# One decoder layer on one core: z and v projections with 512 output columns per matmul instead of 256

## The chip, the cores and the metric

The kernel runs on one core of a Trainium2 chip. The metric is the device time of one execution in microseconds (us). Five engines work side by side, each through its own queue in order: TensorE (PE in the profile, with its weight loads listed apart as PEld), VectorE (DVE), ScalarE (ACT), GpSimd (POOL) and SyncE (SP), which issues most transfers.

## The reference, cut to what matters

One layer of a hybrid decoder, 512 tokens by 1024 features, float32. One input projection of x gives q, k, v of 16 attention heads of 64, the gate z and the inputs x, B, C, dt of a Mamba-2 branch with 32 heads in 4 groups, and two branch gates. The change touches the two products whose results have tokens on the partitions:

```
proj = x @ w_in[l]
q, k, v, f_logit, z, xbc, dt_raw, gate_logit = jnp.split(proj, split_idx, axis=-1)
...
u = (y.reshape(bsz, seq, SSM_INNER) * jax.nn.silu(z.astype(jnp.float32))).reshape(bsz, seq, SSM_GROUPS, -1)
...
return jnp.einsum('bhqk,bhkd->bhqd', p, vh)
```

z has 2048 columns, 512 for each of the four Mamba groups; v has 1024 columns, 64 for each head. Behind the two branches come an output projection, a LayerNorm, a SwiGLU feed-forward part and a second LayerNorm.

## The kernel before

Each operand of a large product is split into hi + lo (float32r), and a product is three matmuls, hi·hi, hi·lo, lo·hi (`mm3`, lines 97 to 100), summed in PSUM. Weights come in chunks of 1024 values per partition: a transfer on SP's queue into `raw` (4 buffers), a copy on ACT that makes `whi`, a subtraction on DVE that makes `wlo` (3 buffers each; `load_w`, lines 85 to 95, both with high priority in the scheduler).

There are three forms of product. `gemm_ws` holds weights in the array and streams 512 tokens; it serves x, B, C, q, k, the gates and the feed-forward up and gate projections. `gemm_down` holds activations and streams 512 weight columns, one PSUM bank for each of the token tiles (128 tokens). `gemm_xs` (lines 118 to 132) also holds activations, but streams 256 weight columns; two token tiles share one PSUM bank, and it runs twice (`pair` 0 and 1) for the 512 columns of a Mamba group's z, and once for the 256 columns of v of four heads.

PSUM has eight banks: a ring `gps` of 3 for projections and a ring `cps` of 5 for transposes, scores and small products.

A scheduler sets the order of each engine's queue ahead of time. The stages: x is transposed tile by tile along with z of group 0; small parameters; B, C and x of group 0; for each group g a chain `group_y` (scan over four chunks) beside the projections of its neighbours, then z of group g (`group_z`, lines 248 to 257: tanh on ACT, one multiply on DVE per bank into `gz`), then `group_u` (lines 315 to 331: for each token tile y times gz, a sum of squares on ACT, a power on POOL, a scaling by DVE, four transposes on PE, a split). Then attention by groups of four heads (hg): q and k of the next group are projected (`att_qk`) while the heads of this group run, v of the group stands ahead of its heads (`att_v`, lines 370 to 379). A head (`att_head`) is scores (lines 390, 391) on PE, maximum (395) on DVE, exponential (397) on ACT, reciprocal and scaling (398, 399) on DVE, transposes (412) on PE, a split on ACT and DVE (65, 66), and the product with v (418) on PE. Rings of few buffers join the steps: the score bank, the transposed bank and the output bank all come from `cps`.

Of the kernel before, what the change touches and what calls it, by code (L numbers as in the profile page):

```python
# [9 lines left out]
F32 = mybir.dt.float32  # L10
F32R = mybir.dt.float32r
BF16 = mybir.dt.bfloat16
AF = mybir.ActivationFunctionType
ALU = mybir.AluOpType
# [23 lines left out]
def tile_hybrid_decoder_layer(  # L38
# [6 lines left out]
    """Operands of the large products are split exactly as hi + lo (float32r each); a product is  # L45
    hi*hi + hi*lo + lo*hi, accumulated in float32."""
# [21 lines left out]
    def gps():  # L68
        return psum.tile([P, T], F32, name="gps", bufs=3)

    def cps():
        return psum.tile([P, T], F32, name="cps", bufs=5)

    # SBUF slots by size (KB), shared over the phases of the layer
# [10 lines left out]
    def load_w(src, a, b, dst=None):  # L85
        """Weights [a * 128, b] to SBUF, split; hi and lo of each block of 128 rows."""
        raw = stream.tile([P, 1024], F32, name="raw", bufs=4)
        nc.sync.dma_start(out=raw.rearrange("p (a b) -> p a b", a=a), in_=src.rearrange("(a p) c -> p a c", p=P))
        if dst is None:
            dst = ([stream.tile([P, 1024], F32R, name="whi")], [stream.tile([P, 1024], F32R, name="wlo")])  # L90
        n = 1024 // len(dst[0])
        with tc.high_priority():
            for i, (hi, lo) in enumerate(zip(*dst)):
                split(hi, lo, raw[:, i * n:(i + 1) * n])
        return [[t[:, j * b:(j + 1) * b] for t in part for j in range(n // b)] for part in dst]
# [9 lines left out]
    def gemm_ws(w, c0, nk, rhs, evac, alloc=gps, n=T, chunks=None):  # L105
        """256 output features (two blocks of 128 partitions) x n tokens; weights stationary."""
# [11 lines left out]
    def gemm_xs(w, c0, lhs, evac, before=None):  # L118
        """512 tokens x 256 output features, tokens on partitions; activations stationary."""
        ps = [gps() for _ in range(2)]  # L120
        for half in range(2):
            hi, lo = ws_chunk(w, c0, half)
            for tt in range(NT):
                if before is not None and half == 0:
                    before(tt)
                o = ps[tt // 2][:, (tt % 2) * 256:(tt % 2 + 1) * 256]
                for k in range(4):
                    kt = half * 4 + k
                    mm3(o, lhs(kt, tt), (hi[k], lo[k]),
                        kt == 0 and tt % 2 == 0, kt == KD - 1 and tt % 2 == 1)  # L130
        for i in range(2):
            evac(i, ps[i].rearrange("p (t c) -> p t c", t=2))
# [4 lines left out]
    def gemm_down(chunk, nk, lhs, tts, half, evac, alloc, tail=0, tail_dst=None):  # L137
        """Tokens tts x 512 output features, tokens on partitions; the last `tail` pairs of k token by token."""
# [18 lines left out]
    def new_act():  # L157
        """A [1024 features, 512 tokens] operand: features on partitions, hi and lo."""
# [8 lines left out]
    def transpose_in(a, src, tt):  # L167
        """Token tile src [128 tokens, 1024] into the operand a."""
# [79 lines left out]
    def group_z(g, before=None):  # L248
        gz = big("gz")
        for pair in range(2):  # L250
            def evac(i, ps, pair=pair):
                th = slot("th").rearrange("p (t c) -> p t c", t=2)
                nc.scalar.activation(out=th, in_=ps, func=AF.Tanh, scale=0.5)
                nc.vector.scalar_tensor_tensor(out=gz[:, 2 * i:2 * i + 2, pair * 256:(pair + 1) * 256], in0=th,
                                               scalar=1.0, in1=ps, op0=ALU.add, op1=ALU.mult)
            gemm_xs(w_in, C_Z + g * 512 + pair * 256, lhs_x, evac, before if pair == 0 else None)
        return gz

    def group_y(g, st):
# [8 lines left out]
        for c in range(NT):  # L268
# [5 lines left out]
            for hf in range(2):  # L274
                # exp(min(acum[l] - acum[s], 0)) * cb[l, s], zero where l < s
# [94 lines left out]
    def att_v(hg):  # L370
        vt = slot("xtok", (P, NT, 4, P), F32R)

        def evac(i, ps):
            sv = ps.rearrange("p t (h d) -> p t h d", h=4)
            hi = vt[:, 2 * i:2 * i + 2, :, 0:64]
            nc.scalar.copy(out=hi, in_=sv)
            nc.vector.tensor_tensor(out=vt[:, 2 * i:2 * i + 2, :, 64:128], in0=sv, in1=hi.bitcast(F32), op=ALU.subtract)
# [3 lines left out]
    def att_head(h, qk, vt, of):  # L381
# [4 lines left out]
        for i in range(NT):  # L386
# [7 lines left out]
            # pt = -(s + mask), with its least value: the negated maximum  # L394
# [109 lines left out]
    # log1p(exp(-|v|)) = 2 atanh(s), s = e / (2 + e) <= 1/3  # L504
# [96 lines left out]
    for hg in range(4):  # L601
# [3 lines left out]
        vt = att_v(hg)  # L605
# [142 lines left out]
    banks = [gps(), gps(), gps(), cps()]  # L748
# [30 lines left out]
```

## Time and profile before

| what | value |
|---|---|
| median of three runs | 1175.7 us (1175.45 to 1175.77) |
| span of the profiled execution | 1171.8 us |
| time of the runs around that span | 3.9 us (1175.7 - 1171.8); the profiled execution's own time is not given apart |
| PE busy | 1145.6 us, 98% |
| DVE busy | 679.9 us, 58% |
| ACT busy | 468.4 us, 40% |
| POOL busy | 99.1 us, 8% |
| DMA | 112.66 MB, 96 GB/s |

The busy time of PE is the union of its matmuls, whose ends are modelled and overlap: a matmul listed with 0.39 us may be followed by the next 0.23 us after its start. So distances from start to start are the measure of what a matmul costs, not its listed duration.

### The profile page before, as it was taken

The numbers are of one execution on the slowest core, as the hardware profiler recorded it, in microseconds if no ns is written. First come the engines' busy times: TensorE is split into PE (matmuls) and PEld (weight loads), VectorE is DVE, ScalarE is ACT, GpSimd is POOL, SyncE is SP. The second block draws the span as 40 slices with busy tenths as digits, with TensorE's granted clock in tenths as the row PEclk, the third lists the DMA queues.
The fourth block names the chain that finished last, engine by engine and source line by source line (L and its number), as shares of the span: only waits on it lengthen the run. The fifth ranks groups of instructions, "written<-read, shape, count | busy, mean of one in ns | idle before, by whom it ended". The sixth has DMA issues, their size and how long they took to land.

```text
span 1171.8 us, 15180 instructions
## 1 busy us (share of the span) xinstructions
PE 1145.6 (98%) x5966; PEld 959.3 (82%) x5966; DVE 679.9 (58%) x1110; ACT 468.4 (40%) x826; POOL 99.1 (8%) x137
## 2 busy tenths in 40 slices
PE   7999999999999999999999999999999999999997
PEld 6887779879778888888787888888888888888886
DVE  3579964883786565877878344546443433432426
ACT  3376763453442434655656352302322322322120
POOL 2003130030131001120200000010000000000001
PEclk9999999999999999999999999999999999999999
DMA  8343243233231232222221355502333333333221
GB/s 244 90 129 126 73 126 90 74 117 100 83 99 55 91 90 73 57 72 73 56 73 55 90 162 161 169 31 72 108 90 105 94 92 106 90 100 98 91 72 73
DMA packets 99576, 112.66 MB, mean 96 GB/s; under 512 B 4820, under 2 KB 84912, under 8 KB 99376
## 3 DMA queue, kind: packets, MB, share of 16 engines
q1 hardware_dynamic: 97024, 107.03, 30.6%
q10 hardware_dynamic: 1152, 4.19, 1.0%
q0 software_dynamic: 1328, 0.46, 0.3%
q8 instruction: 47, 0.77, 0.3%
q14 instruction: 25, 0.20, 0.1%
HBM read 109.38 MB, written 2.16 MB: 95 GB/s over the span
## 4 chain that ended last, share of the span: by engine, by line
PE 86%; DVE 7%; ACT 2%; POOL 2%; issue 2%; DMA 1%; SPq 0%; DVEq 0%; ACTq 0%; POOLq 0%
PE gps L100 20%; PE gps L98 20%; PE gps L99 20%; PE cps L98 6%; PE cps L100 6%; PE cps L99 6%; PE cps L418 1%; PE cps L287 1%; PE cps L412 1%; DMA raw<-in_w_in_dram 1%; DVE wlo L66 1%; DVE t_ul L66 1%; PE cps L244 1%; PE cps L296 1%; PE cps L304 1%
## 5 line engine op out<-in xcount | busy, mean ns | idle before, releaser
L66 DVE TENSOR_TENSOR wlo<-raw,whi 128x1024 fp32r<-128x1024 f32 x171 | 210.1, 1228 | 316.6 <-ACT whi L65 316.5
L65 ACT CAST whi<-raw 128x1024 fp32r<-128x1024 f32 x171 | 179.6, 1050 | 401.2 <-PE gps L99 134.3
L99 PE MATMUL gps<-xl,whi 128*128 128x512 f32 (+1 forms) x648 | 253.6, 391 | 0.0
L98 PE MATMUL gps<-xh,whi 128*128 128x512 f32 (+1 forms) x648 | 252.6, 390 | 0.1
L100 PE MATMUL gps<-xh,wlo 128*128 128x512 f32 (+1 forms) x648 | 251.6, 388 | 0.0
L98 PEld LDWEIGHTS gps<-xh,whi 128*128 128x128 f32 x648 | 122.1, 188 | 23.3 <-issue 0.7
L100 PEld LDWEIGHTS gps<-xh,wlo 128*128 128x128 f32 x648 | 122.4, 189 | 21.9
L99 PEld LDWEIGHTS gps<-xl,whi 128*128 128x128 f32 x648 | 122.2, 189 | 21.6 <-issue 0.2
L98 PE MATMUL gps<-whi,xh 128*128 128x256 f32 (+1 forms) x400 | 116.1, 290 | 2.7 <-ACT xh L65 2.7
L99 PE MATMUL gps<-wlo,xh 128*128 128x256 f32 (+1 forms) x400 | 115.8, 290 | 0.2 <-DVE wlo L66 0.2
L100 PE MATMUL gps<-whi,xl 128*128 128x256 f32 (+1 forms) x400 | 115.9, 290 | 0.0
L98 PEld LDWEIGHTS gps<-whi,xh 128*128 128x128 f32 x400 | 77.4, 194 | 4.3 <-ACT xh L65 3.5
L99 PEld LDWEIGHTS gps<-wlo,xh 128*128 128x128 f32 x400 | 77.4, 193 | 1.4 <-DVE wlo L66 0.5
L100 PEld LDWEIGHTS gps<-whi,xl 128*128 128x128 f32 x400 | 77.4, 194 | 0.6
L98 PE MATMUL cps<-xh,whi 128*128 128x512 f32 (+1 forms) x176 | 66.8, 380 | 0.0
L100 PE MATMUL cps<-xh,wlo 128*128 128x512 f32 (+1 forms) x176 | 66.8, 379 | 0.0
L99 PE MATMUL cps<-xl,whi 128*128 128x512 f32 (+1 forms) x176 | 66.8, 379 | 0.0
L676 POOL TENSOR_TENSOR mv<-mv,neghalf 128x1 f32<-128x1 f32 x8 | 9.2, 1154 | 569.8 <-DVE mv L675 569.8
L198 DVE SCALAR_TENSOR_TENSOR t_v<-gps,cw,t_v 128x511 f32<-128x511 f32 (+2 forms) x72 | 53.4, 744 | 4.3 <-ACT t_v L195 3.5
L100 PE MATMUL gps<-t_uh,wlo 128*128 128x512 f32 x128 | 51.4, 402 | 0.0
L99 PE MATMUL gps<-t_ul,whi 128*128 128x512 f32 x128 | 51.0, 398 | 0.3 <-DVE t_ul L66 0.3
L98 PE MATMUL gps<-t_uh,whi 128*128 128x512 f32 x128 | 50.3, 393 | 0.0
(560 smaller groups left out, 1913.2 us busy)
## 6 DMA issues: line engine op xcount, KB each, us to landing
raw<-in_w_in_dram SPq DMA_DIRECT2D x80, 512.0 KB, 3.7
raw<-in_w_ffn_gate_dram SPq DMA_DIRECT2D x22, 512.0 KB, 3.8
raw<-in_w_ffn_up_dram SPq DMA_DIRECT2D x22, 512.0 KB, 3.8
raw<-in_w_ffn_down_dram SPq DMA_DIRECT2D x22, 512.0 KB, 3.8
t_ab<-ac_d SPq DMA_DIRECT2D x32, 256.0 KB, 3.3
raw<-in_w_proj_ssm_dram SPq DMA_DIRECT2D x16, 512.0 KB, 3.5
raw<-in_w_out_dram SPq DMA_DIRECT2D x8, 512.0 KB, 3.9
raw<-in_w_proj_attn_dram SPq DMA_DIRECT2D x8, 512.0 KB, 4.2
```

Of the source, the lines that this page charges most:

```text
L65: nc.scalar.copy(out=hi, in_=src)
L66: nc.vector.tensor_tensor(out=lo, in0=src, in1=hi.bitcast(F32), op=ALU.subtract)
L98: nc.tensor.matmul(out=o, lhsT=l[0], rhs=r[0], start=start, stop=False)
L99: nc.tensor.matmul(out=o, lhsT=l[0], rhs=r[1], start=False, stop=False)
L100: nc.tensor.matmul(out=o, lhsT=l[1], rhs=r[0], start=False, stop=stop)
L198: nc.vector.scalar_tensor_tensor(out=v[:, sh:], in0=ps[:, 0:T - sh], scalar=cw[:, k, blk:blk + 1], in1=v[:, sh:], op0=ALU.mult, op1=ALU.add)
L244: nc.tensor.transpose(out=pt[:, c * P:(c + 1) * P], in_=xst[:, c * P:(c + 1) * P], identity=ident)
L287: nc.tensor.matmul(out=py[:, r * 64:(r + 1) * 64], lhsT=ms[r // 4][:, r % 4, :], rhs=xdt[:, r * 64:(r + 1) * 64], start=True, stop=True)
L296: nc.tensor.matmul(out=po, lhsT=cT[:, cs], rhs=hprev, start=True, stop=True)
L304: nc.tensor.matmul(out=pst, lhsT=btok[:, cs], rhs=xw, start=True, stop=True)
L412: nc.tensor.transpose(out=ps[:, o:o + P], in_=pr[i][:, kb * P:(kb + 1) * P], identity=ident)
L418: nc.tensor.matmul(out=po[:, kb * P:], lhsT=vt[:, kb, hh, :], rhs=pT[kb][j], start=kb == 0 and j == 0, stop=kb == NT - 1 and j == 1)
```

## The change

`gemm_xs` takes four `gps` banks, one for each token tile, and streams 512 weight columns from chunks of 256 rows by 512 columns (four chunks in place of two passes of two chunks). Each token tile is handed to its eviction as soon as its last matmul is issued. `group_z` calls it once instead of twice. `att_v` makes v of eight heads at once, into two `xtok` slots, for hg 0 and hg 2; hg 1 and hg 3 use the second slot. The rings become 4 `gps` and 4 `cps`, and the last product takes four `gps` banks. Comment lines go, which shifts line numbers by 2 to 3 (412 becomes 411, 418 becomes 417).

```diff
     def gps():
-        return psum.tile([P, T], F32, name="gps", bufs=3)
+        return psum.tile([P, T], F32, name="gps", bufs=4)
     def cps():
-        return psum.tile([P, T], F32, name="cps", bufs=5)
+        return psum.tile([P, T], F32, name="cps", bufs=4)
...
     def gemm_xs(w, c0, lhs, evac, before=None):
-        ps = [gps() for _ in range(2)]
-        for half in range(2):
-            hi, lo = ws_chunk(w, c0, half)
+        ps = [gps() for _ in range(NT)]
+        for kc in range(KD // 2):
+            hi, lo = load_w(w[kc * 256:(kc + 1) * 256, c0:c0 + T], 2, T)
             for tt in range(NT):
-                if before is not None and half == 0:
+                if before is not None and kc == 0:
                     before(tt)
-                o = ps[tt // 2][:, (tt % 2) * 256:(tt % 2 + 1) * 256]
-                for k in range(4):
-                    kt = half * 4 + k
-                    mm3(o, lhs(kt, tt), (hi[k], lo[k]),
-                        kt == 0 and tt % 2 == 0, kt == KD - 1 and tt % 2 == 1)
-        for i in range(2):
-            evac(i, ps[i].rearrange("p (t c) -> p t c", t=2))
+                for k in range(2):
+                    kt = kc * 2 + k
+                    mm3(ps[tt], lhs(kt, tt), (hi[k], lo[k]), kt == 0, kt == KD - 1)
+                if kc == KD // 2 - 1:
+                    evac(tt, ps[tt])
...
-        for pair in range(2):
-            def evac(i, ps, pair=pair):
-                th = slot("th").rearrange("p (t c) -> p t c", t=2)
...
+        def evac(tt, ps):
+            th = slot("th")
+            nc.scalar.activation(out=th, in_=ps, func=AF.Tanh, scale=0.5)
+            nc.vector.scalar_tensor_tensor(out=gz[:, tt, :], in0=th, scalar=1.0, in1=ps, op0=ALU.add, op1=ALU.mult)
+        gemm_xs(w_in, C_Z + g * 512, lhs_x, evac, before)
...
     def att_v(hg):
-        vt = slot("xtok", (P, NT, 4, P), F32R)
+        vt = [slot("xtok", (P, NT, 4, P), F32R) for _ in range(2)]
+        def evac(tt, ps):
+            sv = ps.rearrange("p (h d) -> p h d", h=8)
+            for i in range(2):
+                hi = vt[i][:, tt, :, 0:64]
+                nc.scalar.copy(out=hi, in_=sv[:, 4 * i:4 * i + 4])
+                nc.vector.tensor_tensor(out=vt[i][:, tt, :, 64:128], in0=sv[:, 4 * i:4 * i + 4], in1=hi.bitcast(F32), op=ALU.subtract)
...
-        vt = att_v(hg)
+        if hg % 2 == 0:
+            vts = att_v(hg)
+        vt = vts[hg % 2]
...
-    banks = [gps(), gps(), gps(), cps()]
+    banks = [gps() for _ in range(4)]
```

The order of the queues moves with it. The first place is DVE's queue at the end of z of group 1, where `gz` is made (254, now 252) and `group_u` begins (320, 323, 325, now 317, 320, 322; `t_y` is the scan's output, `ss` the sum of squares). Before, from the third of the four z evictions on:

```order
L254 SCALAR_TENSOR_TENSOR t_gz_1584<-t_th_1811,gps_1701 128x2x256
L320 SCALAR_TENSOR_TENSOR t_y_1318<-t_y_1318,t_gz_1584 128x512
L320 SCALAR_TENSOR_TENSOR t_y_1355<-t_y_1355,t_gz_1584 128x512
L323 TENSOR_SCALAR ss_1820<-ss_1820 128x1
L325 SCALAR_TENSOR_TENSOR t_y_1318<-t_y_1318,ss_1820,t_nw_791 128x512
L323 TENSOR_SCALAR ss_1834<-ss_1834 128x1
L325 SCALAR_TENSOR_TENSOR t_y_1355<-t_y_1355,ss_1834,t_nw_791 128x512
L66 TENSOR_TENSOR wlo_1975<-raw_1972,whi_1974 128x1024
L254 SCALAR_TENSOR_TENSOR t_gz_1584<-t_th_1814,gps_1702 128x2x256
```

Now, from the first of the four evictions on:

```order
L252 SCALAR_TENSOR_TENSOR t_gz_1488<-t_th_1595,gps_1489 128x512
L317 SCALAR_TENSOR_TENSOR t_y_1222<-t_y_1222,t_gz_1488 128x512
L252 SCALAR_TENSOR_TENSOR t_gz_1488<-t_th_1604,gps_1490 128x512
L317 SCALAR_TENSOR_TENSOR t_y_1259<-t_y_1259,t_gz_1488 128x512
L252 SCALAR_TENSOR_TENSOR t_gz_1488<-t_th_1613,gps_1491 128x512
L320 TENSOR_SCALAR ss_1628<-ss_1628 128x1
L317 SCALAR_TENSOR_TENSOR t_y_1222<-t_y_1222,t_gz_1488 128x512
L322 SCALAR_TENSOR_TENSOR t_y_1222<-t_y_1222,ss_1628,t_nw_695 128x512
L66 TENSOR_TENSOR wlo_1783<-raw_1780,whi_1782 128x1024
L252 SCALAR_TENSOR_TENSOR t_gz_1488<-t_th_1622,gps_1492 128x512
```

Before, two evictions stood half a projection earlier, each for two token tiles; now all four stand at the end, each followed by the multiply of its own token tile. In PE's queue the four groups of transposes behind z stood after 5, 2, 22 and 13 matmuls each, and stand after 8, 15, 1 and 2 now.

The second place is PE's queue from the product with v of head 0 (418, now 417) to the scores of head 1 (390 and 391, now 389 and 390; names `t_bT`, `t_xst`, `t_cT`, `t_xdt` are head 1's k and q). Before:

```order
L418 MATMUL cps<-t_uh,t_xtok 128x512
L390 MATMUL cps<-t_bT,t_xst 128x128
L391 MATMUL cps<-t_cT,t_xdt 128x128
L418 MATMUL cps<-t_uh,t_xtok 128x512
L418 MATMUL cps<-t_uh,t_xtok 128x384
L390 MATMUL cps<-t_bT,t_xst 128x256
L391 MATMUL cps<-t_cT,t_xdt 128x256
```

Now:

```order
L417 MATMUL cps<-t_uh,t_xtok 128x512
L99 MATMUL gps<-xl_81,whi 128x512
L100 MATMUL gps<-xh_79,wlo 128x512
L417 MATMUL cps<-t_uh,t_xtok 128x512
L417 MATMUL cps<-t_uh,t_xtok 128x384
L389 MATMUL cps<-t_bT,t_xst 128x128
L417 MATMUL cps<-t_uh,t_xtok 128x384
L417 MATMUL cps<-t_sq,t_xtok 128x256
L390 MATMUL cps<-t_cT,t_xdt 128x128
L417 MATMUL cps<-t_sq,t_xtok 128x256
L417 MATMUL cps<-t_uh,t_xtok 128x128 x2
L389 MATMUL cps<-t_bT,t_xst 128x256
```

With four `cps` banks the next head's first scores stand behind three of the eight products with v instead of one, and its second scores behind all eight.

The third place is PE's queue where the heads of hg 0 end (`t_xw` and `t_ul` are head 3's weights, `gps_4419` and now `gps_4062` the last k projection of hg 1). Before:

```order
L98 MATMUL gps_4419<-xh1_80,whi_4452 128x512
L418 MATMUL cps_4314<-t_xw_4294,t_xtok_3931 128x256
L418 MATMUL cps_4314<-t_ul_4293,t_xtok_3931 128x128 x2
L99 MATMUL gps_4419<-xl1_82,whi_4452 128x512
L100 MATMUL gps_4419<-xh1_80,wlo_4453 128x512
L98 MATMUL gps_4509<-whi_4513,xh0_79 128x256
L99 MATMUL gps_4509<-wlo_4514,xh0_79 128x256
```

Now:

```order
L417 MATMUL cps_3957<-t_ul_3936,t_xtok_3547 128x128 x2
L98 MATMUL gps_4062<-xh1_80,whi_4095 128x512
L99 MATMUL gps_4062<-xl1_82,whi_4095 128x512
L100 MATMUL gps_4062<-xh1_80,wlo_4096 128x512
L389 MATMUL cps_4152<-t_v_4123,t_btok_4033 128x128
L390 MATMUL cps_4152<-t_th_4124,t_cbm_4034 128x128
```

Before, the 96 matmuls of v for hg 1 came next and the scores of head 4 behind them; now the scores of head 4 follow at once, and the first transpose of head 4 stands behind 25 matmuls counted from head 3's last transposes. In PE's queue everything behind the last head of hg 3 stands as before.

## Rows read from the trace of the kernel before

**Rows 1.** The page, parts 1 and 2: busy time; granted clock in tenths of full.
```profile
PE 1145.6 (98%) x5966; PEld 959.3 (82%) x5966; DVE 679.9 (58%) x1110; ACT 468.4 (40%) x826; POOL 99.1 (8%) x137
PEclk9999999999999999999999999999999999999999
```

**Rows 2.** Groups by line and shape, PE: one of three alike, z and v.
```profile
L98 PE MATMUL gps<-whi,xh 128*128 128x256 f32 x384 | 109.8, 286 | 2.7 <-ACT xh L65 2.7
```

**Rows 3.** Timeline of PE, z of group 1: first and last of 97 matmuls.
```profile
177.75 0.28 PE L99 MATMUL gps<-wlo,xh 128*128 128x256 f32 x1
...
189.27 0.28 PE L99 MATMUL gps<-wlo,xh 128*128 128x256 f32 x1
```

**Rows 4.** Timeline of PE, down projection: first and last of 134 matmuls.
```profile
1059.77 0.39 PE L100 MATMUL cps<-whi,t_uh 128*128 128x512 f32 x1
...
1089.91 0.39 PE L98 MATMUL cps<-whi,t_y 128*128 128x512 f32 x1
```

**Rows 5.** Busy time by stretch: z of group 1, then the down projection.
```profile
core 0: us, PE busy (x) PEld busy (x) DVE busy (x) ACT busy (x) POOL busy (x), PEclk, DMA share, GB/s
178.00:189.00 11.00, 11.00 (x94) 11.00 (x93) 3.36 (x4) 3.19 (x4) 0.00 (x0) 1.00 0.33 97
1060.00:1090.00 30.00, 30.00 (x134) 24.86 (x133) 6.97 (x6) 6.33 (x6) 0.00 (x0) 1.00 0.31 97
```

**Rows 6.** Waits, longest first: us in total, times, longest.
```profile
PEld cps L412 <- DVE t_y L399: 6.1, 20, 0.5
...
PE cps L329 <- DVE t_y L325: 2.5, 6, 0.7
...
PE cps L329 <- DVE ss L323: 1.6, 3, 0.5
```

**Rows 7.** Timeline of PE and ACT, start: x is transposed, first z.
```profile
9.65 0.41 PE L98 MATMUL gps<-whi,xh 128*128 128x256 f32 x1
...
11.36 0.41 PE L100 MATMUL gps<-whi,xl 128*128 128x256 f32 x1
...
18.51 0.28 PE L98 MATMUL gps<-whi,xh 128*128 128x256 f32 x1
18.63 0.28 PE L99 MATMUL gps<-wlo,xh 128*128 128x256 f32 x1
...
13.78 1.04 ACT L65 CAST whi<-raw 128x1024 fp32r<-128x1024 f32 x1 [3.53 <-DMA raw<-in_w_in_dram]
```

**Rows 8.** Busy time by stretch (columns as in rows 5): heads of hg 1, then v.
```profile
503.80:544.00 40.20, 39.92 (x214) 31.76 (x212) 33.91 (x98) 25.11 (x59) 8.12 (x16) 1.00 0.22 65
544.00:555.60 11.60, 11.60 (x97) 11.52 (x97) 7.24 (x10) 4.88 (x7) 0.00 (x0) 1.00 0.29 83
```

**Rows 9.** Groups by line and shape, DVE, 452 to 650 us: attention.
```profile
L66 DVE TENSOR_TENSOR wlo<-raw,whi 128x1024 fp32r<-128x1024 f32 x23 | 28.1, 1224 | 7.6 <-ACT whi L65 7.6
L66 DVE TENSOR_TENSOR t_ul<-cps,t_ul 128x512 fp32r<-128x512 f32 x16 | 10.3, 681 | 1.7 <-ACT t_ul L65 1.6
L395 DVE CUSTOM_DVE_ANT_0 t_y<-cps,mneg 128x384 f32<-128x384 f32 x16 | 8.7, 544 | 0.0
L377 DVE TENSOR_TENSOR t_xtok<-gps,t_xtok 128x512 fp32r<-128x512 f32 x8 | 5.5, 687 | 4.8 <-ACT t_xtok L376 4.8
L365 DVE SCALAR_TENSOR_TENSOR t_th<-gps,t_v 64x512 fp32r<-64x512 f32 x6 | 4.1, 682 | 0.1
L66 DVE TENSOR_TENSOR t_sq<-cps,t_sq 128x256 fp32r<-128x256 f32 x8 | 3.3, 412 | 0.0
L364 DVE CAST t_th<-t_v 64x512 fp32r<-64x512 f32 x6 | 2.5, 421 | 0.3
```

**Rows 10.** Groups by line and shape, DVE, 190 to 210 us: end of z.
```profile
L325 DVE SCALAR_TENSOR_TENSOR t_y<-t_y,ss,t_nw 128x512 f32<-128x512 f32 x4 | 3.0, 750 | 2.1 <-POOL ss L324 2.1
L320 DVE SCALAR_TENSOR_TENSOR t_y<-t_y,t_gz 128x512 f32<-128x512 f32 x4 | 2.6, 684 | 0.0
L254 DVE SCALAR_TENSOR_TENSOR t_gz<-t_th,gps 128x512 f32<-128x512 f32 x2 | 1.4, 683 | 1.2 <-ACT t_th L253 1.2
```

More of the change, by code (lines that the diff above doesn't have):

```diff
@@ L249, in group_z @@
         gz = big("gz")
-        for pair in range(2):
-            def evac(i, ps, pair=pair):
-                th = slot("th").rearrange("p (t c) -> p t c", t=2)
[L253 to L256, printed above, removed]
+        def evac(tt, ps):
[3 more added lines that the diff above has]
+        gemm_xs(w_in, C_Z + g * 512, lhs_x, evac, before)
         return gz
@@ L370, in att_v @@
     def att_v(hg):
-        vt = slot("xtok", (P, NT, 4, P), F32R)
[L373 to L377, printed above, removed]
+        vt = [slot("xtok", (P, NT, 4, P), F32R) for _ in range(2)]
[5 more added lines that the diff above has]
+                nc.vector.tensor_tensor(out=vt[i][:, tt, :, 64:128], in0=sv[:, 4 * i:4 * i + 4], in1=hi.bitcast(F32), op=ALU.subtract)
         gemm_xs(w_in, C_V + hg * 256, lhs_x, evac)
```

## The prediction, on record before the result

> **What bounds the kernel now.** I read the page first. PE is busy in 98% of the span and its granted clock stands at the top level in all slices [rows 1]. So PE's own time bounds the kernel, and an edit pays by what it takes off PE, less what it leaves PE waiting. The listed duration of a matmul overlaps the next, so I then read the distance from start to start off the timeline, in a stretch of each of the two forms that hold activations and stream weights. The 256-column form: 96 distances from 177.75 to 189.27 us, 11.52 / 96 = **0.1200 us** each [rows 3]. The 512-column form, in the down projection: 133 distances from 1059.77 to 1089.91 us, 30.14 / 133 = **0.2266 us** [rows 4]. Two matmuls of 256 columns cost 0.2400, one of 512 does the same work in 0.2266: 0.0134 us less a pair. In both stretches PE is busy without a gap; in the 256 stretch the weight loads too are busy all the time, 11.00 of 11.00 us, in the 512 stretch 24.86 of 30.00 [rows 5]. The small forms pay a fixed part for each weight load and the large ones pay it half as often. Last I read the waits of PE and the busy time by stretch where the order of the queues changes.
>
> **The matmuls.** z and v before are three groups of 384 matmuls of 256 columns [rows 2], 1152; after, 576 of 512. 1152 x 0.1200 - 576 x 0.2266 = 138.2 - 130.5 = **7.7 us** less on PE. The down projection also walks through four banks of PSUM with the same 2 x 512 chunks, so it is the changed form already running, and I take its pitch unchanged. The Trainium skill ("TensorE: Matmul & The Clock Gate", section "Back-to-back issue gap") gives a warm gap of N / 2.4 GHz plus about 2.5 ns. By it the pair would cost 218.3 ns against 215.8, and the change 576 x 2.5 ns = 1.4 us. The trace does not agree: 120.0 and 226.6 ns are 13.3 ns above N / 2.4 in both forms. The sum goes by the rows.
>
> **The cold start.** Until 18.5 us matmuls of z stand 0.214 us apart ((11.36 - 9.65) / 8), then 0.12 [rows 7]: that is 256 columns at 1.2 GHz, after a stretch in which PE mostly waited, though the clock column shows 1.00 there. At that level 512 columns should cost two times 256, so the pairs issued before 18.5 us save nothing. About 18 matmuls, 9 pairs x 0.0134 = 0.1 us, to be taken off. What ends the waits there is ACT's copy of the second weight chunk, which waits for its transfer until 13.78 us and stands ahead of the copies of the second token tile [rows 7]; in the new queues it stands there too. Chunks with runs of 512 columns move somewhat more cheaply (0.31 against 0.33 of the DMA engines at the same 97 GB/s [rows 5]); with two of the six transfers before it, that is a few tenths earlier at most. Against it, the transposes of the last token tile now stand behind matmuls of twice the length. Bounds -0.5 and +1.0 us, I take 0.
>
> **The end of z, three times.** PE waits here for `group_u`: 2.5 + 1.6 = 4.1 us for groups 1 to 3, 1.4 each [rows 6]. After the change the first token tile is complete 18 matmuls (4.1 us) before z ends, and DVE then has four gz, four y x gz, four scalings, one lo part and one weight split: 4 x 0.683 + 4 x 0.684 + 4 x 0.750 + 0.68 + 1.22 = 10.4 us, plus some 2 us of waits for POOL as before [rows 9, 10]. It ends about 8.3 us behind z. PE gets to the last transposes after 26 matmuls, 5.9 us, and three groups of transposes. So PE waits between 0 and 2.4 us, where before it was 1.4: I take no difference, with bounds -1.4 and +1.0 for each of the three.
>
> **Heads without a v block ahead of them, hg 1 and hg 3.** Here a cover goes. The heads of hg 1 and the v block behind them keep DVE busy for 33.91 + 7.24 = 41.2 us of 51.8 [rows 8]. Two weight splits and two lo parts of v, 3.8 us [rows 9], belong to v; the rest, 37.3 us, is heads and q, k. The v block let DVE finish what the heads left. With no block between hg 0 and hg 1, PE spends 40.2 us on a stretch in which DVE has 37.3 us of work: DVE at 93%, no longer 84%. What would be late first is head 4's first transpose. From head 3's last scaling to head 4's first, DVE's new queue holds three pairs of a q copy and a q split (3 x 1.10), three lo parts of head 3 (0.68 + 0.68 + 0.41), one weight split (1.22), two of 0.68 (head 3's output and its lo part), and three maxima of at most 0.54 with small reads and reciprocals (2.1 together, my estimate): 3.30 + 1.77 + 1.22 + 1.36 + 2.1 = **9.8 us** [rows 9]. PE has 25 matmuls in the same piece of its queue, 25 x 0.2266 = 5.7 us, and with them head 3's product with v and head 4's scores. Their price: the heads phase of 40.2 us [rows 8] holds 96 matmuls of q and k, 21.8 us, which leaves 4.6 us a head for all the rest, most of which lies in this piece. So PE takes **9 to 10 us**. They meet. Before, PE had 20 small waits at these transposes, 0.5 us at most [rows 6], so it ran just in time too. I take 0.3 us lost at each of two boundaries, **0.6 us**; bounds 0 and, if DVE kept only the 84% it reached, 37.3 / 0.84 - 40.2 = 4.2 us each.
>
> **Costs taken as nothing.** v is evicted in 16 pieces of 256 columns on each engine instead of 8 of 512: on DVE 16 x 0.41 - 8 x 0.687 = 1.1 us more [rows 9]. The pieces lie beside the v block, where DVE was busy 7.24 of 11.60 us [rows 8], and the first product with v stands behind head 0's transposes; without that cover 1.1 us would show. z takes all four `gps` banks, so its third and fourth token tile need the banks of the product ahead; those are wanted 12 and 18 matmuls, 2.7 and 4.1 us, into z, and one eviction is 0.7 us. The last product takes a `gps` bank for a `cps` bank, the same form. Behind the last head PE's queue is unchanged.
>
> **Sum.** -7.7 + 0.1 + 0.6 = **-7.0 us**. On the profiled execution, 1171.8 to 1164.8 us of span; the 3.9 us around the span stay, and the median goes from 1175.7 to **1168.7 us**, 0.6%. About 0.2%, 2.4 us, is what a measurement of this kernel can tell from no change.
>
> **Rivals.**
> (a) *Part is given back in the heads.* The boundaries cost 2 to 5 us in all. For it: DVE at 93%. Against it: the new queue puts more matmuls ahead of head 4's transposes than ahead of head 0's (16 against 12), and pulls matmuls of the next v in at hg 1's end. Time: 1170.5 to 1173.3.
> (b) *No gain that can be measured.* Both boundaries at their upper bound, 8.4 us in place of 0.6: 1176.5; from 5.3 us on the result is inside 0.2%. Beside it a smaller one: z's 512 columns come at twice the pitch of 256, 0.2400, because whatever sits between two matmuls grows with the columns; then nothing is gained on PE, about 1176.4. Rows 3 and 4 speak against it, since both forms stand there side by side. The page of the Trainium skill named above comes near it: by its section 1.4 us would be left to gain.
> (c) *Slower: the ring of four for scores and transposes.* The next head's first scores now stand behind three products with v, and the second behind all eight, since their bank is one that the transposes held until the lo part was split off. If the chain of a head (scores, maximum, exponential, scaling, transposes, split, product) ends each head, it grows by about one split, 0.68 us [rows 9], in 16 heads: 10.9 us, 1179.6. For it: the transposes were just in time. Against it: in 1171.8 us PE's waits for scaled scores add up to 6.1 us on the load side only [rows 6], and matmuls of projections stand between. It decides from 0.6 us a head on.
> (d) *The change does not do what it says*: PE's new queue holds the matmuls with 512 columns, so this is left at nothing.
>
> **How the numbers follow.** The forecast 0.68, with its own range 1167.2 to 1170.5 (the bounds of start and z); (a) 0.15; (b) 0.10, of which 0.02 is the smaller one; (c) 0.07. The range for 8 in 10 reaches into (a): 1166.9 to 1172.8, which leaves out (b), (c) and the ends. Faster is the forecast and (a), and a little of (b) that falls short of 5.3 us: 0.84; same 0.09; slower 0.07.
>
> **What would show it.** The distance from start to start in z and v: 0.226 to 0.227 us, in 576 matmuls of 512 columns; if it is 0.235 or more, the pitch was wrong. PE's waits at z's ends: about 4 us in three groups. The two stretches of eight heads: about 2 x 40.2 + 0.3 us from the first scores of hg 0 to the next v, less the 11 matmuls of v pulled in; DVE there at 90% or more. Longer starts of head 4's and head 12's transposes, with DVE's scaling (398) as releaser, would show (a); a lasting wait of scores for a bank, or PE's busy share under 97% through all 16 heads, would show (c). A median above 1173.4 would make the forecast wrong, and then the heads are the first place to look.

## The result and the profile after

The changed kernel takes 1167.99 us (median of 4 executions, 1167.74 to 1168.29), the kernel before 1175.58 (4 executions beside it): ratio **0.9939**, 95% interval 0.9925 to 0.9953. A second measurement on one chip gave 1168.33 against 1175.35 (0.9945, 0.9931 to 0.9958). The forecast was 1168.7. The traced execution took 1168.29 us with a span of 1166.6.

The page of the changed kernel, its parts 1, 2 and 5 (the group is one of three alike, z and v with 16 other matmuls of that form):

```profile
PE 1140.0 (98%) x5390; PEld 926.4 (79%) x5390; DVE 680.6 (58%) x1118; ACT 468.9 (40%) x834; POOL 102.8 (9%) x137
...
PEclk8999999999999999999999999999999999999999
...
L98 PE MATMUL gps<-whi,xh 128*128 128x512 f32 x208 | 82.7, 398 | 4.4 <-ACT xh L65 4.4
```

PE has 576 instructions fewer than in [rows 1], as the diff says; its clock column has an 8 in the first slice, which was a 9. The timeline of PE, z of group 1 from its first matmul to the first one behind it:

```profile
174.15 0.39 PE L98 MATMUL gps<-whi,xh 128*128 128x512 f32 x1
...
195.91 0.39 PE L98 MATMUL gps<-xh,whi 128*128 128x512 f32 x1
```

(195.91 - 174.15) / 96 = **0.2267 us**, the distance of [rows 4], where [rows 3] gave 0.1200 for half the columns. The waits (us in total, times, longest):

```profile
PEld cps L411 <- DVE t_y L398: 11.4, 37, 0.8
...
PE cps L326 <- DVE t_y L322: 3.8, 6, 0.7
...
PEld cps L389 <- DVE sm L394: 2.3, 5, 0.6
```

Against [rows 6]: PE's waits at the ends of z are 3.8 us in all, 4.1 before. The load side (PEld, the loading of weights into the array) waits 11.4 us in all for scaled scores, where it was 6.1, and the last row is new: scores wait until DVE has taken the maximum out of the bank that they need.

The starts of the products in PE's timeline cut the span in stretches. Two executions of each kernel (the second column is a further trace of before, at 1175.66 us the usual time; the fourth a further one of after, 1168.30 us):

```
us                                     before   before, later   after   after, later
start of the span to z of group 1      174.76   176.79          174.15  174.15
  of it z of group 0                    32.57    33.07           33.00   31.60
z of groups 1, 2 and 3                  69.09    69.10           65.27   65.28
between these three                    152.24   152.31          152.14  152.18
end of z of group 3 to first v          47.34    47.33           47.38   47.37
first v to the attention projection    267.33   267.35          266.51  266.50
from there to the last matmul          453.19   453.19          453.24  453.22
last matmul starts at                 1163.95  1166.07         1158.69 1158.70
```

All of the gain lies ahead of the attention projection. Between the usual executions (second and fourth column) it is 7.37 us: 2.64 ahead of z of group 1, 3.82 in the other three z, 0.85 in the attention, 0.06 in the rest. Between the first two traces it was 5.26, because the first execution of before was 2 us quicker than usual, ahead of z of group 1 alone. What happens there differs from one execution to the next; a section below is about it.

### The profile page after: what moved, and what is told of

It is laid out like the page before. It is cut to its first block, busy times and chain, and to the rows that moved or that the text cites. A ratio compares the mean times of both kernels' runs of the same rounds, so it can differ in the third digit from the quotient of the medians.

```text
span 1166.6 us, 14040 instructions
## 1 busy us (share of the span) xinstructions
PE 1140.0 (98%) x5390; PEld 926.4 (79%) x5390; DVE 680.6 (58%) x1118; ACT 468.9 (40%) x834; POOL 102.8 (9%) x137
## 4 chain that ended last, share of the span: by engine, by line
PE 51%; DVE 2%; ACT 0%; issue 0%; POOL 0%; DVEq 0%; ACTq 0%
PE gps L100 11%; PE gps L98 11%; PE gps L99 11%; PE cps L98 5%; PE cps L100 5%; PE cps L99 5%; PE cps L411 1%; PE cps L417 1%; DVE t_sd L682 0%; PE cps L389 0%; PE cps L390 0%; DVE t_sd L670 0%; DVE st L671 0%; PE cps L171 0%; POOL mv L677 0%
## 5 line engine op out<-in xcount | busy, mean ns | idle before, releaser
L98 PE MATMUL gps<-whi,xh 128*128 128x512 f32 x208 | 82.7, 398 | 4.4 <-ACT xh L65 4.4
L100 PE MATMUL gps<-whi,xl 128*128 128x512 f32 x208 | 82.4, 396 | 0.0
L99 PE MATMUL gps<-wlo,xh 128*128 128x512 f32 x208 | 82.3, 396 | 0.0
L98 PEld LDWEIGHTS gps<-whi,xh 128*128 128x128 f32 x208 | 39.7, 191 | 13.6 <-ACT xh L65 5.0
L99 PEld LDWEIGHTS gps<-wlo,xh 128*128 128x128 f32 x208 | 39.7, 191 | 8.6 <-DVE wlo L66 0.5
L100 PEld LDWEIGHTS gps<-whi,xl 128*128 128x128 f32 x208 | 39.6, 190 | 8.4 <-DVE xl L66 0.3
```

The lines of the kernel that those rows point to most:

```text
L98: nc.tensor.matmul(out=o, lhsT=l[0], rhs=r[0], start=start, stop=False)
L99: nc.tensor.matmul(out=o, lhsT=l[0], rhs=r[1], start=False, stop=False)
L100: nc.tensor.matmul(out=o, lhsT=l[1], rhs=r[0], start=False, stop=stop)
```

## The experiments

### The kernel before, twice more

The first without any edit, to set an execution's time beside its span.

> The kernel before once more, unchanged, to see one execution's time beside its own span. The traced execution of before had a span of 1171.8 us, 3.9 us under the median; the changed kernel's runs have only 1.7 us around the span (1168.29 against 1166.6). Theory A (the trace of before shows an execution that was faster than the median): time minus span is 1.7 us again, and with a median near 1175.6 us the span is near 1173.9, so that the change took 7.3 us off the span of the usual execution and not 5.2. Theory B (something around the span got shorter with the change): time minus span is 3.9 us, span 1171.8.

Measured: 1173.6 us with a span of 1171.9, 1.7 us apart: theory A. The 3.9 us that the prediction put around the span were wrong; the traced execution of before must have taken about 1173.5 us. Twenty executions of before beside it lay between 1172.9 and 1177.5 us.

> The kernel before for one more trace. Both traces of it so far are of executions near 1173.6 us, where half of its executions take 1175 us or more. If this one is slower, theory L says that all of its surplus lies ahead of z of group 1 (at 174.8 us in both traces), as 0.43 us a matmul of 512 columns near 64 to 68 us or as a longer wait near 117 to 120 us; the stretches from there on are those of the two traces within 0.3 us. Rival: the surplus lies in the heads or is spread over the whole span.

Measured: 1175.66 us, and theory L holds for it: the surplus of 2.03 us is there when z of group 1 starts, and every later stretch is within 0.1 us of the first trace. Where it arises is seen in the timeline of PE in this third execution of before. `cps<-t_y` are running sums of the gate terms:

```profile
61.88 0.29 PE L538 MATMUL cps<-t_y,tri 128*128 128x16 f32 x2
...
63.81 0.37 PE L538 MATMUL cps<-t_y,tri 128*128 128x16 f32 x2
64.03 0.48 PE L100 MATMUL gps<-xh,wlo 128*128 128x512 f32 x1
...
65.08 0.63 PE L100 MATMUL gps<-xh,wlo 128*128 128x512 f32 x1
65.50 0.63 PE L98 MATMUL gps<-xh,whi 128*128 128x512 f32 x1
```

Behind two microseconds of matmuls with 16 columns, matmuls of 512 stand 0.42 us apart in place of 0.227: the lower of the clock's two levels, 1.2 in place of 2.4 GHz. The busy time by stretch of this execution and then of the first trace of before (the number behind the engines is the granted clock):

```profile
core 0: us, PE busy (x) PEld busy (x) DVE busy (x) ACT busy (x) POOL busy (x), PEclk, DMA share, GB/s
16.00:20.00 4.00, 4.00 (x23) 3.77 (x22) 3.25 (x6) 2.50 (x4) 0.00 (x0) 0.59 1.04 379
...
64.00:68.00 4.00, 4.00 (x15) 2.76 (x15) 2.17 (x6) 1.88 (x5) 0.00 (x0) 0.57 0.00 0
```

```profile
16.00:20.00 4.00, 4.00 (x26) 4.00 (x25) 3.70 (x6) 2.54 (x5) 0.00 (x0) 1.00 1.04 377
...
64.00:68.00 4.00, 4.00 (x30) 3.37 (x29) 2.69 (x8) 3.14 (x8) 0.00 (x0) 1.00 0.07 16
```

30 matmul records in four microseconds against 15: near 64 us the first execution of before kept the top level (2.4 GHz). From 16 to 20 us the 1.00 of its row is not to be taken at its word, for its matmuls of 256 columns stood 0.214 us apart until 18.5 us [rows 7], half the top rate. In the third execution they do so for longer:

```profile
19.24 0.41 PE L98 MATMUL gps<-whi,xh 128*128 128x256 f32 x1
19.45 0.41 PE L99 MATMUL gps<-wlo,xh 128*128 128x256 f32 x1
...
20.66 0.28 PE L99 MATMUL gps<-wlo,xh 128*128 128x256 f32 x1
20.78 0.40 PE L100 MATMUL gps<-whi,xl 128*128 128x256 f32 x2
```

So of the 2.03 us, 0.44 are there when PE comes to the running sums (61.36 against 60.92 us), and the rest is added from 64 to 68 us.

### The rings alone, z alone, v alone

The rings, in the kernel before:

```
-        return psum.tile([P, T], F32, name="gps", bufs=3)
+        return psum.tile([P, T], F32, name="gps", bufs=4)
-        return psum.tile([P, T], F32, name="cps", bufs=5)
+        return psum.tile([P, T], F32, name="cps", bufs=4)
```

> The kernel before with rings of 4 and 4 banks, z and v in the old form. Theory (the gain is the distance from start to start of the matmuls): no difference, 1175.6 us, within 1 us. Rival 1 (the ring of four for the products gives part of the gain: the stretch between z of group 0 and z of group 1 became 0.96 us shorter though no product in it was changed): 1174.6 us, and that stretch is shorter here too (133.8 us, not 134.7). Rival 2 (the ring of four for scores and transposes costs time, hidden in the result): 1 to 4 us slower than before, in the stretches of heads.

Measured: 1176.47 us (1174.48 to 1177.99), 1.0011 (1.0001 to 1.0020). Slower by 1.1 us: the theory's "no difference" falls, and so does the time of rival 1; rival 2 holds at its lower bound. From the first v to the attention projection the trace has 268.54 us, 1.21 more than before. A part of rival 1 is in the trace all the same: from the end of z of group 0 to z of group 1 it takes 134.17 us, the first two traces of before 134.73 and 134.53. The waits of this trace, against [rows 6]:

```profile
PEld cps L412 <- DVE t_y L399: 10.2, 30, 0.6
...
PEld cps L390 <- DVE sm L395: 2.9, 6, 0.6
```

The second row has no counterpart in before: with four banks scores stand and wait for the maximum of earlier scores. That this wait makes the 1.21 us is likely, but not shown by itself.

z alone (rings 4 and 4, `att_v` and its matmuls as before):

> The changed kernel with v in the old form, four heads at a time; z with 512 columns; rings 4 and 4. Theory: three groups of z save 1.3 us each, group 0 nothing (its matmuls stay at 0.427 us, 1.2 GHz, until 21.7 us, where before they left that level at 18.5), and the stretches of heads are those of before: 1175.6 - 3.8 = 1171.8 us; with the 0.96 us of rival 1 above 1170.8. Rival (most of what v gave back in the stretches of heads is the rings' doing and not the missing v block): the stretches of heads are longer than before here too, 1173 us or more.

Measured: 1170.40 us (1170.13 to 1171.44), 0.9960 (0.9947 to 0.9972). That is 0.4 us below the theory's lower figure, and the rival's 1173 falls. The rival's mechanism is half right, though: the attention takes 268.55 us, as with the rings alone, so the stretches of heads are longer than before without any change to v.

v alone (rings 4 and 4, `group_z` and its matmuls as before):

> The changed kernel with z in the old form; v with 512 columns, eight heads at a time; rings 4 and 4. Theory (the v block saves 2.6 us on the matmuls, and 1.7 us of it are given back because the transposes of heads 4 to 7 and 12 to 15 wait for the scaled scores without a v block ahead): 1175.6 - 0.9 = 1174.7 us, with 11 us of waits for scaled scores on the load side as in the changed kernel. Rival (nothing is given back; what is missing in the changed kernel is lost elsewhere): 1173.0 us. The two parts should add up to the whole change, -7.6 us, if they don't touch one another.

Measured: 1174.24 us (1171.98 to 1176.01), 0.9990 (0.9980 to 1.0000): near the theory. The attention takes 266.53 us, as in the changed kernel, with 11.4 us of waits for scaled scores. The traced execution, 1175.34 us, had the clock's fall near 64 us (0.57 from 64 to 68 us). On medians, rings +1.1; z on top of them 1170.40 - 1176.47 = -6.1; v on top of them 1174.24 - 1176.47 = -2.2: together -7.2, where the whole change has -7.0 and -7.6.

### Halves: the distance between matmuls

The changed kernel, each matmul of 512 columns in two:

```
-                    mm3(ps[tt], lhs(kt, tt), (hi[k], lo[k]), kt == 0, kt == KD - 1)
+                    for f in range(2):
+                        fs = slice(f * 256, (f + 1) * 256)
+                        mm3(ps[tt][:, fs], lhs(kt, tt), (hi[k][:, fs], lo[k][:, fs]),
+                            kt == 0 and f == 0, kt == KD - 1 and f == 1)
```

> The changed kernel in which each matmul of z and v with 512 columns is two of 256 into the halves of the same bank; order of chunks, rings and evictions as in the changed kernel. Theory (the gain is the distance from start to start): 576 x (2 x 0.1200 - 0.2266) = 7.7 us more, less what the cold start hides, so 1168.0 + 6.0 to 7.7 = 1174.0 to 1175.7 us, distance 0.120 us again. Rival (the gain comes from the order of chunks, the fewer evictions of z or the v block for eight heads): 1168 to 1170 us.

Measured: 1175.83 us, 1.0006 (0.9996 to 1.0016) against before, so 7.5 to 7.8 us above the changed kernel. The theory holds, 0.1 us above its range: order, rings and evictions without the longer matmul gain nothing in sum. In the trace a z takes 23.03 us again and the first v of eight heads too (21.76 with 512 columns; the second stands among matmuls of the heads, and is counted with the same figure here). Without its two v blocks the attention takes 222.99 us here and in the changed kernel alike (269.05 - 2 x 23.03, 266.51 - 2 x 21.76), in before 267.33 - 4 x 11.51 = 221.29. So the heads lose **1.7 us** to order and rings, whatever the matmuls of v do; 1.33 of them lie ahead of the heads of hg 2 (79.50 us without v against 78.17). The rule on the gap of an isolated matmul (the Trainium skill, "TensorE: Matmul & The Clock Gate", section "Back-to-back issue gap") would, as an estimate, have left 1.4 us between halves and whole; the runs, with 7.5 to 7.8, do not agree with it.

### Where the heads lose 1.7 us

Rings of 3 and 5 again, the fourth token tile of z and v in the other ring:

```
-        ps = [gps() for _ in range(NT)]
+        ps = [gps(), gps(), gps(), cps()]
```

> The changed kernel with rings of 3 and 5 banks again; the fourth token tile of z and v takes its bank from the ring of scores and transposes. Theory (the ring of four costs 1.2 us in the heads: the stretch from the first to the third v block was 90.8 us in both kernels with old v and rings 4 and 4, 89.7 in both runs of the kernel before): 1168.0 - 1.2 = 1166.8 us, and the waits of scores for the maximum before them (1.3 and 1.0 us in the changed kernel) are gone. Rival (a v or z block now holds one bank of that ring for 22 us, which hurts the chain of a group or of the heads beside it): 1168.0 us or more.

Measured: 1168.70 us (1167.64 to 1169.33): the rival. The waits of scores for the maximum are gone, as the theory has it, and the attention without v still takes 223.00 us, as with rings of four. So the ring of four alone (222.50) costs 1.2 us, v for eight heads with rings of 3 and 5 costs 1.7 (223.00), and both together cost no more. In this kernel v and z also borrow a bank of the other ring, so v for eight heads isn't quite alone here. Next, less work for DVE:

```
-                nc.vector.tensor_copy(out=t2[a:a + 64, :], in_=t1[0:64, :].bitcast(F32))
+                (nc.gpsimd if hg % 2 == 1 else nc.vector).tensor_copy(out=t2[a:a + 64, :], ...)
```

> The changed kernel with one of the operations of q and k, the copy of the high part to the other operand, done by GpSimd instead of DVE for heads 4 to 7 and 12 to 15 (16 copies of 0.42 to 0.46 us off DVE). Theory D (in the stretches without a v block DVE is late with the scaled scores; this is where 1.7 us of the v block's 2.6 went): the waits for scaled scores on the load side fall from 11.4 towards 6 us, and 0.8 to 1.7 us are gained, 1166.3 to 1167.2 us beside 1168.0. Rival (the stretch is set by the chain of a head on several engines, and DVE's busy share only goes along): 1167.7 to 1168.5 us. GpSimd's copies may slow DVE down; then the copies and scalings of these stretches take longer in the rows.

Measured: 1168.44 us (1167.49 to 1169.35) beside 1168.33 for the changed kernel on the same chip. The rival: no gain, waits for scaled scores 13.4 us. Busy time (columns as above) in the heads of hg 0 in the kernel before, then from the end of the first v to the start of the next in the changed kernel, and then with the copies on GpSimd:

```profile
454.94:494.01 39.07, 38.84 (x202) 30.64 (x201) 34.15 (x97) 25.37 (x60) 8.15 (x16) 1.00 0.20 56
```

```profile
460.70:538.41 77.71, 76.75 (x393) 59.03 (x392) 68.72 (x196) 51.46 (x121) 16.64 (x32) 1.00 0.19 57
```

```profile
460.06:536.58 76.52, 75.97 (x390) 58.69 (x389) 65.40 (x185) 50.59 (x120) 21.93 (x40) 1.00 0.20 58
```

DVE was busy for 68.72 of 77.71 us, 88%, and for 65.40 of 76.52, 85%, with the copies gone, yet the attention without v took 223.3 us. The stretch is shorter only because the next v starts earlier among the heads' matmuls: from the start of the first v to the end of the second it is 123.27 us, 123.02 in the changed kernel. The copies on GpSimd also got in DVE's way. Three of its sixteen scalings of 256 columns took 675 to 707 ns, the others 337 to 348; those three began while a copy was at work, as the timelines of GpSimd and DVE show for the first:

```profile
483.29 0.77 POOL L361 CAST t_cbm<-t_btok 64x512 fp32r<-64x512 f32 x1 [1.45 <-ACT t_btok L360]
```

```profile
483.50 0.71 DVE L398 TENSOR_SCALAR t_y<-t_y,sm 128x256 f32<-128x256 f32 x1
```

That is about 1 us in all and may hide a small gain, but 5.5 us less work for DVE (132.47 in place of 137.94 us from the first v to the end of the heads, outside the v blocks) gave nothing back. So DVE's amount of work is unlikely to be what binds here, which leaves the chain of a head (scores, maximum, exponential, scaling, transposes, split, product) as the likely cause. It was not tried by itself; which link sets the 1.7 us stays open.

### What happens ahead of z of group 1

z of group 0 in the old form, the rest as changed:

```
-    gz = group_z(0, load_x)
+    gz = group_z256(0, load_x)
```

> The changed kernel with z of group 0 alone in the old form. Theory S (the executions of the kernels with the old z of group 0 lie 4 us apart, those with the new one within 1.3 us, because with the old one PE comes to the stretch of 16-column matmuls near 62 us at such times that the granted clock falls there in some executions): the times spread over 3 us or more, median 1169 to 1171 us. Theory C (512 columns in group 0 cost 1.6 us through the longer wait and the clock that rises at 21.7 instead of 18.5 us, and nothing else changes): 1166.4 to 1168 us within 1 us of each other.

Measured: 1169.47 us (1168.42 to 1169.77). Both theories fall: theory S, since the executions lie within 1.4 us, theory C, since it is 1.1 to 1.5 us slower than the changed kernel. In the traces that difference is a third event. The timelines of ACT in this execution and in the changed kernel's, and PE's in the first:

```profile
118.05 0.40 ACT L305 ACTIVATE t_ab<-t_ab,acum 128x128 f32<-128x128 f32 x1 [1.60 <-DMA t_ab<-ac_d]
```

```profile
116.90 0.40 ACT L278 ACTIVATE t_ab<-t_ab,acum 128x128 f32<-128x128 f32 x1 [0.32 <-DMA t_ab<-ac_d]
```

```profile
121.30 0.94 PE L242 MATMUL cps<-t_cT,t_bT 128*128 128x128 f32 x6 [1.50 <-DVE ss L347]
```

A broadcast from DRAM lands later, ACT stands before it with a weight copy and the tanh of C behind, DVE's C waits, and PE 1.5 us for it (0.21 in the changed kernel's first trace). The delay goes with the old form of z of group 0: PE waits there in all six traces that have it (0.79, 0.47 and 0.77 us in before, 0.62 with the rings alone, 1.57 with v alone, 1.50 here), and 0.21 us at most in the eight that have the new order of chunks, halves among them (0.17). Why its size differs is open.

Next come seven matmuls that nobody reads, where PE waits for the second token tile:

```
+                    if tt == 1:
+                        fill = cps()
+                        for _ in range(7):
+                            nc.tensor.matmul(out=fill, lhsT=lhs(0, 0)[0], rhs=hi[0], start=True, stop=True)
```

> The changed kernel with seven more matmuls of 512 columns, whose result nobody reads, where PE waits for the second token tile (12.1 to 15.6 us). Theory (the clock stays at 1.2 GHz until 21.7 us because PE waited 3.4 us): the distance falls from 0.427 to 0.227 us before 18.5 us, (21.7 - 18.5) / 2 = 1.6 us or more are saved, 1166.4 us, if the level in the later stretches is as in the changed kernel. Rival (the time of the rise is set by something else): the distance falls near 21.7 us as before, 1168.0 us.

The timeline of PE in the changed kernel without them, and then with them (`cps<-whi,xh` are the seven):

```profile
15.55 0.80 PE L98 MATMUL gps<-whi,xh 128*128 128x512 f32 x1 [3.42 <-ACT xh L65]
...
19.13 0.63 PE L100 MATMUL gps<-whi,xl 128*128 128x512 f32 x1
19.56 0.63 PE L98 MATMUL gps<-whi,xh 128*128 128x512 f32 x1
...
22.91 0.40 PE L98 MATMUL gps<-whi,xh 128*128 128x512 f32 x1
23.14 0.39 PE L99 MATMUL gps<-wlo,xh 128*128 128x512 f32 x1
```

```profile
12.20 2.33 PE L129 MATMUL cps<-whi,xh 128*128 128x512 f32 x7
15.23 0.50 PE L98 MATMUL gps<-whi,xh 128*128 128x512 f32 x1 [0.70 <-ACT xh L65]
...
16.94 0.39 PE L98 MATMUL gps<-whi,xh 128*128 128x512 f32 x1
17.17 0.40 PE L99 MATMUL gps<-wlo,xh 128*128 128x512 f32 x1
```

Without them the matmuls are 0.43 us apart at 19.1 still, and 0.23 at 22.9; with them 0.23 at 16.9 already. PE came out of a wait of 3.42 us at the low level, and out of one of 0.70 us near the top one. In the twelve traces without the seven matmuls the level rose for good between 18.4 and 21.4 us, in the two with them at 13.2 and 14.0. z of group 0 takes 31.40 us in place of 33.00, and this execution 1166.48. But three of the five took 1168.06 to 1168.16, so that the median is 1168.06: as the theory has it in two executions, as the rival in three. None of the three was traced; a second trace of the changed kernel points to a reason:

> The changed kernel once more, unchanged, beside the kernel before on one chip. In the traces the change took 5.2 us off the span, in the medians 7.6. Theory L (the traced execution of before was a quick one, 1173.6 us, and single executions of before lie between 1173 and 1177.5 because of events ahead of z of group 1: when the granted clock rises, whether it falls near 64 us, when a broadcast near 117 us lands): executions of the changed kernel lie within 2 us, and the medians are 6 to 8 us apart. Rival (the changed kernel has the same spread and its four runs were quick ones by chance): a spread of 3 us or more, and a median of 1169 to 1171 us.

Measured: 1168.33 us (1167.18 to 1168.49), theory L. The busy time by stretch of its traced execution, and then of the first trace of the changed kernel:

```profile
20.00:24.00 4.00, 4.00 (x22) 3.33 (x20) 1.29 (x2) 2.06 (x3) 0.00 (x0) 1.00 0.77 193
60.00:64.00 4.00, 4.00 (x28) 3.71 (x28) 2.38 (x6) 0.74 (x3) 0.00 (x0) 0.86 0.40 131
64.00:68.00 4.00, 4.00 (x23) 3.06 (x22) 1.18 (x3) 2.04 (x5) 0.00 (x0) 0.71 0.07 16
```

```profile
20.00:24.00 4.00, 4.00 (x20) 3.40 (x19) 1.91 (x4) 1.07 (x2) 0.00 (x0) 0.83 0.81 206
60.00:64.00 4.00, 3.85 (x31) 3.34 (x29) 2.57 (x6) 0.09 (x1) 0.00 (x0) 1.00 0.45 135
64.00:68.00 4.00, 4.00 (x29) 3.36 (x29) 2.56 (x7) 2.78 (x7) 0.00 (x0) 1.00 0.07 16
```

In the second execution (the first three rows) the clock rises early, at 18.5 us, and falls near 64 us; in the first it rises late, at 21.3 by the transposes that run then (the next matmul of 512 columns stands at 21.7), and does not fall. z of group 1 starts at 174.15 us in both. So each pays once, about 1.5 us, where the third execution of before pays 0.4 and 1.6. The last kernel is to take away both. It has the seven matmuls, and the ten matmuls of 16 columns go to three places among the products of group 0, which move with them:

```
-    for tt in range(NT):
-        o = ps[:, 256 + tt * AH:256 + (tt + 1) * AH]
...
     st = group_bc(0)
-    for pair in range(2):
-        group_x(0, st, pair)
+    cum_tt((0, 1))
+    group_x(0, st, 0)
+    cum_tt((2,))
+    group_x(0, st, 1)
+    cum_tt((3,))
```

> The kernel with seven extra matmuls at the start, in which the ten matmuls of 16 columns near 62 us (running sums of the forget terms, wanted only in the attention) are put in three places among the products of group 0. Theory (in the executions at 1168.1 us of the kernel with extra matmuls, the 1.5 us won at the start were lost again because the granted clock fell behind the stretch of 16-column matmuls, as in the second trace of the changed kernel: 0.86 and 0.71 from 60 to 68 us): no fall there in any execution, median 1166.5 us, all within 1 us, z of group 1 starting at or before 172.4 us. Rival (the 1.5 us are lost elsewhere, or the clock falls behind another stretch once this one is gone): median 1167.5 us or more with executions at both levels.

Measured: **1166.80 us** (1166.43 to 1166.89), 0.9925 (0.9911 to 0.9939) against before: the theory within 0.3 us of its figure, though z of group 1 starts at 172.75 us and not by 172.4. All five executions are below all nine of the changed kernel (1167.18 to 1168.49). That none of the five had the fall is seen in the one trace, and argued from the times in the others. Its busy time by stretch:

```profile
16.00:20.00 4.00, 3.34 (x21) 2.48 (x19) 3.27 (x6) 2.61 (x4) 0.00 (x0) 1.00 1.03 383
20.00:24.00 4.00, 4.00 (x22) 3.30 (x21) 1.98 (x3) 2.17 (x3) 0.00 (x0) 1.00 0.81 206
60.00:64.00 4.00, 3.97 (x24) 3.39 (x25) 2.93 (x7) 2.55 (x7) 0.00 (x0) 1.00 0.49 146
64.00:68.00 4.00, 4.00 (x25) 3.33 (x24) 2.32 (x4) 1.17 (x2) 0.00 (x0) 1.00 0.62 168
```

## Why the prediction was right, point by point

- **The matmuls, -7.7 us.** Right in mechanism and size. 0.2267 us was measured, z of groups 1 to 3 gave 3.82 us (3.87 by the step), the v blocks 46.04 - 43.52 = 2.52 (2.57), and cutting the matmuls in halves took the whole gain away. Why a matmul costs 13 ns more than its columns was not tried.
- **The cold start, +0.1.** Near the mark for z of group 0, but the stretch behind it was missing from the sum. By the steps, z of group 0 was to bring 1.29 - 0.1 = 1.2 us. Between two executions whose clock rose at 18.5 us (the first of before and the second of the changed kernel) it brought 32.57 - 31.60 = 0.97. With rises at other times (20.1 us in the third execution of before, 21.3 in the first of the changed kernel) it brings between -0.4 and 1.5 us. What the step missed is that this time, and the clock's fall near 64 us, differ from one execution to the next. The other part is there with and without the clock's fall: from the end of z of group 0 to z of group 1 the changed kernel takes 133.77 us against 134.73 where the clock did not fall, and 135.23 against 136.34 where it did. That is 1.0 to 1.1 us less without any change to a product in it; 0.6 of it is the wait for the broadcast near 120 us (0.21 and 0.16 us in place of 0.79 and 0.77). The sum had no term for it.
- **The end of z, 0.** Right: 3.8 us of waits in place of 4.1, and the stretches between the z within 0.2 us.
- **The heads, +0.6.** The step that failed, in size and in its reason. They lost 1.7 us. The step had DVE at 93% of the stretch; it was busy 88% of it, 87% before (34.15 of 39.07 us), because the 37.3 us of work counted for a heads phase were 34.4. Taking 5.5 us of work off DVE gave nothing back. What sets the 1.7 us in its place stays open.
- **The rings, nothing.** Wrong by themselves: 1.1 us slower, and scores wait for a bank as in rival (c). Its price was 0.68 us in a head; 1.21 / 16 = 0.08 was measured. In the changed kernel this isn't a loss on top of the heads' 1.7, as far as the kernel with rings of 3 and 5 shows it.
- **The sum, -7.0.** -7.6 and -7.0 were measured. Two errors cancel: 1.4 us more ahead of z of group 1, 1.1 us less in the heads. So the mechanism was right, but that the sum came so near is in part luck. That the span's 3.9 us stay, was wrong too (1.7). Nor does the range 1167.2 to 1170.5 follow from its bounds: those of the start and of three z add up to -4.7 and +4.0 us.
- **Rivals.** (a) comes nearest: the heads lost 1.7 us, just under its 2 to 5, with DVE at 88% and not the 93% that it built on, and the gain ahead of z of group 1 kept the time out of its range (by its own costs that range is 1170.1 to 1173.1). (b) is excluded, in its main form by these 1.7 us where it asked for 8.4, in its smaller one by the distance. (c) exists at an eighth of its price. In the list of what would show it, the start distances and the waits at z's ends came as written; DVE at 90% or more did not.

## What to carry to other kernels

Where PE bounds a kernel, a matmul of 512 columns in place of two of 256 is worth the fixed part of one, here 13 ns a pair: read the two distances off stretches that already run side by side, and the sum holds to a few hundredths of a microsecond a block. Before a sum is made against a traced execution, take a second trace: events of 1 to 2 us ahead of the change can hide in a single one. Compare then executions in which the clock rose and fell alike, stretch by stretch. And a ring that gives up a bank has a price in the stretch where its other users are a chain, even where no wait for a bank is seen before.

## What the runs showed of the hardware

- The granted clock fell to 1.2 GHz behind a stretch of ten matmuls with 16 columns, though PE was busy in it (3.85 of the 4.00 us from 60 to 64 us in the third execution of before), and in some executions only: in five of the thirteen traces that have the ten in a row. Matmuls of 512 columns came 0.42 us apart from 64.7 to 67.6 us in one execution of before, 0.23 in another. With the ten in three places no trace or time shows it; other products moved with them, so that they are the cause is likely and not shown by itself.
- The moment at which the clock rises at the start differs between executions of one kernel: behind waits of 3.42 and 2.87 us PE was at 1.2 GHz until 21.3 and until 18.5 us in two traces of the changed kernel. Seven matmuls without a purpose, put into the wait, brought the top level by 16.9 us at the latest. The Trainium skill ("TensorE: Matmul & The Clock Gate", section "Part 1: The HAM clock gate") says that the count of slow matmuls at a kernel's start varies between runs of it; these traces agree.
- The clock column of the first execution of before shows 1.00 from 16 to 20 us, where the distances between matmuls show half the rate until 18.5 us. Distances decide.
- One broadcast from DRAM, issued among weight loads, let PE wait 0.47 to 1.57 us with the old order of the first projection's chunks, and 0.21 us at most with the new one.
- Copies on GpSimd made three of sixteen scalings on DVE last twice as long, 675 to 707 ns in place of 337 to 348: those that began while a copy was at work.
